# A hybrid attention layer: the stick-breaking heads' weights transposed by VectorE squares and a round trip through DRAM instead of by TensorE

## The chip, the cores and the metric

The kernel runs on one core of one Trainium2 chip. The metric is the device time of one execution in microseconds (us); lower is better. The core has TensorE (PE in the profile, its weight loads PEld), VectorE (DVE), ScalarE (ACT), GpSimd (POOL) and SyncE (SP). Each engine works through its own instructions in the order in which they stand in the built program, and starts one when the semaphores that it waits for have been raised. SP computes nothing: it issues nearly all DMAs of this kernel, in order.

## The reference: what is computed

One residual layer over a sequence of 1024 positions with 1024 channels. The input is normalised and modulated, projected to queries, keys, values and gates of 16 heads of 64 channels (8 forgetting heads, 8 stick-breaking heads), each head mixes, the gated head outputs go through one output projection, and a residual and a layer norm end it. Cut to the part that the change touches:

```python
def _stick_breaking_block(q, k, v, q_pos, k_pos):
    scale = HEAD_DIM ** -0.5
    z = jnp.einsum('bhqd,bhkd->bhqk', q, k).astype(jnp.float32) * scale
    strict = k_pos[None, :] < q_pos[:, None]
    log_beta = jax.nn.log_sigmoid(z)
    log_keep = jnp.where(strict, jax.nn.log_sigmoid(-z), 0.0)
    later = lax.cumsum(log_keep, axis=3, reverse=True) - log_keep
    w = jnp.where(strict, jnp.exp(log_beta + later), 0.0)
    return jnp.einsum('bhqk,bhkd->bhqd', w.astype(v.dtype), v)
```

The weights `w` come out with the queries on the partitions; the product with `v` sums over keys, so it needs the keys on the partitions. Each 128x128 block of `w` must be transposed.

## The kernel before, in words

Everything is fp32 split into a high part (fp32r) and a low remainder, and a product is made of high and low terms. After a start that computes modulation and the first projections, the program is a list of 128 units `u = (p, h, i)`: head pair `p` of 0 to 7 (0 to 3 are the stick-breaking heads), head `h` of the pair, and block `i` of 128 queries, which sees `(i + 1) * 128` keys (`ke`). This stretch of 64 stick-breaking units, from the first scores at 88.8 us to the last, is called the stage here.

One stick-breaking unit goes through these steps (line numbers are those of the profile of before):

- `att_scores`: the scores `S` on PE (L427, L428), into one PSUM tile that has no second buffer; `kp` and `be`, two sigmoids on ACT (L447, L448); a running product from the right over `kp` on DVE (L453, and L457 for more than 512 keys); the product `be * kp` on POOL (L461). `kp` and `be` are SBUF tiles of one pool of six buffers, so three units can hold theirs at a time.
- `att_transpose`, called LAG = 2 units later: for each group `g` of up to four key blocks, the blocks of `be` are transposed by PE into a PSUM tile `T` (L478), ACT copies it to the high part `hi` (L480, the "cast" of this text), and DVE subtracts to get the low part `lo` (L481).
- `att_pv`, when both units of a pair of query blocks (2j, 2j+1) are there: the product with `v` on PE (L493), the sum of its halves by ACT and DVE (L512, L513), the gate on POOL (L514), and a store to `y_dr` issued by SP (L522).

Between the units PE works on "fillers": the projections of the next pairs (L270 to L272 for queries, keys and gates, L327 to L329 for values), cut in small steps and dealt out evenly over the units by the table FILL. PE's order is written out by hand: within `pe_order` every PE instruction stands where the program's loop puts it. The orders of ACT, DVE, POOL and SP are made by a scheduler that simulates a timeline. SP issues in this stage the loads of the weights for the fillers (`raw`, L121), the copies of the keys to the other half of the partitions (L252), and the stores of `y_dr` (L522).

The loop that sets the order:

```python
    for k in range(len(units) + LAG + 1):
...
                att_scores(units[k], units[k + 1] if k + 1 < len(units) else None)
...
        fill(want[2 * k + LEAD + 1])
        while ready:
            att_pv(*ready.pop(0))
        if LAG <= k < len(units) + LAG:
            u = units[k - LAG]
            att_transpose(u)
```

Of the kernel before, what the change touches and what calls it, by code (L numbers as in the profile page):

```python
# [27 lines left out]
def tile_hybrid_layer(  # L28
# [17 lines left out]
    nc = tc.nc  # L46
# [4 lines left out]
    dr = ctx.enter_context(tc.tile_pool(name="dr", bufs=1, space=bass.MemoryType.DRAM))  # L51
# [39 lines left out]
    causal = cp.tile([P, P], F32, tag="causal", name="causal")  # L91
# [17 lines left out]
    y_dr = dr.tile([NPAIR, P, SEQ], F32, tag="y_dr", name="y_dr")  # L109
    wo_dr = dr.tile([2, NPAIR, P, D], F32, tag="wo_dr", name="wo_dr")  # L110
    f_dr = dr.tile([8, SEQ], F32, tag="f_dr", name="f_dr")

    def raw_tile(name):
        return sb.tile([P, 528], F32, tag="wraw", bufs=2, name=name)
# [129 lines left out]

    def evac_k(p, ch, acc, kst, klo, heads):
        s = slice(ch * 512, ch * 512 + 512)
        for h in heads:
            r = slice(h * HD, h * HD + HD)
            o = slice((1 - h) * HD, (1 - h) * HD + HD)
            first = nc.scalar.copy(kst[h][r, s], acc[r, :])  # L250
            kf = kst[h].bitcast(F32)
            nc.sync.dma_start(kf[o, s], kf[r, s])  # L252
            if p not in CASTS_FIRST:
                last = nc.vector.tensor_tensor(klo[r, s], acc[r, :], kf[r, s], op=ALU.subtract)
        if p in CASTS_FIRST:
            for h in heads:
                r = slice(h * HD, h * HD + HD)
                last = nc.vector.tensor_tensor(klo[r, s], acc[r, :], kst[h].bitcast(F32)[r, s], op=ALU.subtract)  # L258
        return first, last

    def evac_g(p, ch, acc, sg):
# [12 lines left out]
    qst, kst, klo, sgt, vt = {}, {}, {}, {}, {}  # L274
# [91 lines left out]
    def forget_rows(lf):  # L366
        scratch = att_tile("fscratch")
        tri, fr = scratch[:, :P], scratch[:64, P:2 * P]
        nc.gpsimd.memset(tri, 1.0)
        nc.gpsimd.affine_select(out=tri, in_=tri, pattern=[[1, P]], base=0,  # L370
                                channel_multiplier=-1, compare_op=ALU.is_ge, fill=0.0)
        fp = t_tile("fcum")
        nc.tensor.matmul(fp[:, 64:129], ones.to_broadcast([P, P]), flf, start=True, stop=True)
        nc.tensor.matmul(fp[:, :64], tri, lf, start=True, stop=True)
        pre = fsb.rearrange("p h t -> p (h t)")
        nc.vector.tensor_tensor_scan(pre, fp[:, 64:128], later.rearrange("p h t -> p (h t)"), initial=0.0,
                                     op0=ALU.add, op1=ALU.mult)
# [6 lines left out]
        nc.sync.dma_start(f_dr.rearrange("h (t p) -> (h t) p", p=P), fr)  # L384
        yield

    fb = {}
# [7 lines left out]
    floor, ps_causal = [], []  # L395
# [11 lines left out]
    def att_causal(u):  # L407
        p, h, i = u
        if p >= 4:
            f = fb[2 * (p - 4) + h]  # L410
            dg = slice(i * P, i * P + P)
            nc.vector.tensor_tensor(f[:, dg], f[:, dg], ps_causal[0][:, :P] if ps_causal else causal, op=ALU.add)

    def att_scores(u, following):
        p, h, i = u
        z = zq.pop(u)
        ke = (i + 1) * P
        ns = 1 if ke <= 512 else 2
        w = ke // ns
        qs = slice(i * P, i * P + P)  # L420
        dg = slice(ke - P, ke)
        if p >= 4:
            f = fb[2 * (p - 4) + h]
        S = s_tile(f"S_{p}_{h}_{i}")
        for s in range(ns):
            ks = slice(s * w, s * w + w)
            nc.tensor.matmul(S[:, s, :w], qst[p][h][:, qs], kst[p][h][:, ks], start=True, stop=False)  # L427
            nc.tensor.matmul(S[:, s, :w], z, klo[p][:, ks], start=False, stop=True)  # L428
        v3 = lambda a: a[:, :ke].rearrange("p (a b) -> p a b", a=ns)
        if p >= 4:  # L430
            a = att_tile(f"a_{p}_{h}_{i}")
            nm = sb.tile([P, 1], F32, tag="nm", bufs=4, name=f"nm_{p}_{h}_{i}")
            l = sb.tile([P, 1], F32, tag="l", bufs=4, name=f"l_{p}_{h}_{i}")
            rows = nc.vector.tensor_tensor_reduce(out=v3(a), in0=S[:, :ns, :w], in1=v3(f),  # L434
                                           op0=ALU.add, op1=ALU.min, scale=-1.0, scalar=BIG,
                                           accum_out=nm)
# [5 lines left out]
            nc.gpsimd.tensor_scalar(a[:, :ke], a[:, :ke], l, 1.0, op0=ALU.mult, op1=ALU.mult)  # L442
            st_w[u] = a
        else:
            kp = att_tile(f"kp_{p}_{h}_{i}")
            be = att_tile(f"be_{p}_{h}_{i}")
            nc.scalar.activation(v3(kp), S[:, :ns, :w], AF.Sigmoid, scale=-1.0)  # L447
# [5 lines left out]
            scan = nc.vector.tensor_tensor_scan(rv, rv, floor[0][:, 512 - n:][:, ::-1], initial=0.0,  # L453
                                                op0=ALU.mult, op1=ALU.max)
            if ke > n:
                rv = kp[:, :ke - n][:, ::-1]
                scan = nc.vector.tensor_tensor_scan(rv, rv, floor[0][:, 0:1].to_broadcast([P, ke - n]),  # L457
                                                    initial=kp[:, ke - n:ke - n + 1], op0=ALU.mult, op1=ALU.max)
            with after(scan):
                att_causal(following)  # L460
            nc.gpsimd.tensor_tensor(be[:, :ke - 1], be[:, :ke - 1], kp[:, 1:ke], op=ALU.mult)  # L461
            nc.gpsimd.memset(be[:, ke - 1:ke], 0.0)
            st_w[u] = be

    def att_transpose(u):
        p, h, i = u
# [638 lines left out]
```

## Time and profile before

| | |
|---|---|
| median of 3 runs | 685.24 us (685.07 to 685.33) |
| the profiled execution | 685.25 us, span of its trace 683.5 us |
| PE, PEld busy | 98 %, 86 % of the span |
| DVE, ACT, POOL busy | 66 %, 56 %, 63 % |
| granted TensorE clock, mean | 0.999 |
| DMA moved | 81.60 MB, mean 119 GB/s |
| the stage of the 64 stick-breaking units | about 88.8 to 342.9 us |

Busy time is that of instructions at work; waiting, semaphores and the issuing of DMAs do not count. PE's matmuls overlap in the pipeline, so the duration of one is longer than what it adds in a row of many. A row of the timeline gives start, duration, engine, line, operation, what it writes and reads, and in brackets how long the engine had been idle and which instruction released it. A DMA row has the time that SP needs to issue it, and its landing is when the semaphore is raised that tells of its data.

### The profile page before, as it was taken

Reading aid. Unit: us, or ns where it says so; the run is one execution under the profiler, and the core shown is the slowest. Engines: PE = TensorE matmul, PEld = TensorE weight load, DVE = VectorE, ACT = ScalarE, POOL = GpSimd, SP = SyncE. Lnnn points to the kernel's source line nnn. Section 1 sums busy time; section 2 is a strip of 40 time slices with the busy share of each in tenths; the row PEclk is TensorE's granted clock in tenths of the full one; section 3 lists DMA queues with packets and bytes.
Section 4 is the critical chain, followed back from the end, with each engine's and each line's share of the span. In section 5 each row is a group of like instructions: output and inputs, shape, how many; then the busy total and the mean of one; then the engine's idle time right before and its main releaser. Section 6 shows DMA issues by size and latency. Waiting matters only on the chain.

```text
span 683.5 us, 11770 instructions
## 1 busy us (share of the span) xinstructions
PE 667.2 (98%) x4021; PEld 587.2 (86%) x4021; DVE 450.6 (66%) x914; ACT 382.0 (56%) x861; POOL 427.7 (63%) x558
## 2 busy tenths in 40 slices
PE   5999999999999999999999999999999999999995
PEld 4789898888998888889988888899988889888885
DVE  6785368867666667676675665765566677774645
ACT  5668357856567666566675564655565667531000
POOL 5558977756348566556388896877584364665411
PEclk9999999999999999999999999999999999999999
DMA  9966231112102121122144563453341298143301
GB/s 338 410 236 233 82 105 44 41 29 60 29 9 86 27 57 54 37 55 55 55 131 136 172 176 121 143 166 129 101 150 40 72 327 318 58 162 118 123 31 62
DMA packets 45036, 81.60 MB, mean 119 GB/s; under 512 B 5232, under 2 KB 18864, under 8 KB 44976
## 3 DMA queue, kind: packets, MB, share of 16 engines
q1 hardware_dynamic: 43536, 76.63, 33.8%
q10 hardware_dynamic: 1440, 4.21, 2.2%
q8 instruction: 32, 0.52, 0.3%
q14 instruction: 28, 0.23, 0.1%
HBM read 60.34 MB, written 16.29 MB: 112 GB/s over the span
## 4 chain that ended last, share of the span: by engine, by line
PE 94%; DMA 3%; DVE 2%; ACT 0%; issue 0%; POOL 0%; DVEq 0%
PE m L270 10%; PE m L272 10%; PE m L271 10%; PE pv L493 10%; PE T L478 9%; PE S L428 5%; PE S L427 5%; PE o L884 4%; PE o L882 4%; PE o L883 4%; PE v L327 4%; PE v L328 4%; PE v L329 4%; DMA raws<-in_w_qkg_dram 2%; PE st_late L589 1%; PE st_q L589 1%
## 5 line engine op out<-in xcount | busy, mean ns | idle before, releaser
L270 PE MATMUL m<-uh,whi 128*128 128x512 f32 x304 | 126.4, 416 | 0.0
L272 PE MATMUL m<-uh,wlo 128*128 128x512 f32 x304 | 119.7, 394 | 0.0
L271 PE MATMUL m<-ul,whi 128*128 128x512 f32 x304 | 119.7, 394 | 0.0
L481 DVE TENSOR_TENSOR pt<-T,pt 128x512 fp32r<-128x512 f32 (+2 forms) x192 | 100.5, 550 | 17.5 <-ACT pt L480 16.5
L461 POOL TENSOR_TENSOR be<-be,kp 128x127 f32<-128x127 f32 (+3 forms) x64 | 77.2, 1207 | 33.1 <-DVE kp L457 23.5
L480 ACT CAST pt<-T 128x512 fp32r<-128x512 f32 (+2 forms) x192 | 85.8, 480 | 16.1 <-PE T L478 12.5
L453 DVE TENSOR_TENSOR_SCAN kp<-kp,floor 128x512 f32<-128x512 f32 (+2 forms) x64 | 65.2, 1018 | 31.2 <-ACT kp L447 30.1
L493 PEld LDWEIGHTS pv<-pt,v 128*128 128x128 f32 (+1 forms) x640 | 77.1, 163 | 4.4 <-DVE pt L481 0.7
L493 PE MATMUL pv<-pt,v 128*128 128x256 f32 (+3 forms) x640 | 80.4, 271 | 0.5 <-DVE pt L481 0.5
L442 POOL TENSOR_SCALAR a<-a,l 128x1024 f32<-128x1024 f32 (+3 forms) x64 | 48.1, 751 | 40.3 <-DVE l L441 26.7
L272 PEld LDWEIGHTS m<-uh,wlo 128*128 128x128 f32 x304 | 57.1, 188 | 13.6
L440 ACT ACTIVATE a<-a,nm 128x1024 f32<-128x1024 f32 (+3 forms) x64 | 49.8, 778 | 33.8 <-DVE nm L434 32.7
L427 PE MATMUL S<-k,q 128*128 128x512 f32 (+5 forms) x192 | 66.5, 348 | 0.2 <-DVE nm L434 0.2
L428 PE MATMUL S<-kl,qz 128*128 128x512 f32 (+5 forms) x192 | 65.5, 342 | 0.0
L270 PEld LDWEIGHTS m<-uh,whi 128*128 128x128 f32 x304 | 57.3, 188 | 8.5 <-DVE kl L258 0.2
L271 PEld LDWEIGHTS m<-ul,whi 128*128 128x128 f32 x304 | 57.4, 189 | 8.0
L434 DVE CUSTOM_DVE_ANT_0 a<-S,fb 128x1024 f32<-128x1024 f32 (+3 forms) x64 | 48.3, 755 | 20.1 <-PE S L428 9.3
L514 POOL TENSOR_TENSOR ty<-ty,sg 64x256 f32<-64x256 f32 x64 | 47.5, 742 | 22.3 <-DVE ty L513 11.1
L447 ACT ACTIVATE kp<-S 128x128 f32<-128x128 f32 (+3 forms) x64 | 41.7, 652 | 31.6 <-PE S L428 29.4
L327 PE MATMUL v<-whi_v,uh 128*128 128x256 f32 (+1 forms) x192 | 56.0, 292 | 0.0
L405 ACT CAST qz<-q 64x128 fp32r<-64x128 f32 x128 | 37.4, 295 | 33.2 <-PE S L428 31.8
L328 PE MATMUL v<-whi_v,ul 128*128 128x256 f32 (+1 forms) x192 | 54.2, 282 | 0.0
(285 smaller groups left out, 1593.6 us busy)
## 6 DMA issues: line engine op xcount, KB each, us to landing
raw<-in_w_qkg_dram SPq DMA_DIRECT2D x38, 256.0 KB, 2.9
wss<-in_w_ss_dram SPq DMA_DIRECT2D x16, 512.0 KB, 8.4
x<-in_x_dram SPq DMA_DIRECT2D x8, 512.0 KB, 6.9
k<-k SPq DMA_DIRECT2D x32, 128.0 KB, 2.3
wg<-in_w_gate_dram SPq DMA_DIRECT2D x8, 512.0 KB, 4.9
raw_o<-in_w_out_dram SPq DMA_DIRECT2D x16, 256.0 KB, 2.8
fb<-f_dr ACTq DMA_DIRECT2D x8, 512.0 KB, 4.3
wo_dr<-whi_o SPq DMA_DIRECT2D x16, 256.0 KB, 2.5
```

Source lines behind the costliest of these rows:

```text
L270: nc.tensor.matmul(acc, hi[:, c], u_hi[kt][:, s], start=(kt == 0), stop=False)
L271: nc.tensor.matmul(acc, hi[:, c], u_lo[kt][:, s], start=False, stop=False)
L272: nc.tensor.matmul(acc, lo[:, c], u_hi[kt][:, s], start=False, stop=(kt == NB - 1))
L327: nc.tensor.matmul(acc[:, :n], u_hi[kt][:, ts_], hi[:, s], start=(kt == 0), stop=False)
L328: nc.tensor.matmul(acc[:, :n], u_lo[kt][:, ts_], hi[:, s], start=False, stop=False)
L427: nc.tensor.matmul(S[:, s, :w], qst[p][h][:, qs], kst[p][h][:, ks], start=True, stop=False)
L428: nc.tensor.matmul(S[:, s, :w], z, klo[p][:, ks], start=False, stop=True)
L453: scan = nc.vector.tensor_tensor_scan(rv, rv, floor[0][:, 512 - n:][:, ::-1], initial=0.0, op0=ALU.mult, op1=ALU.max)
L461: nc.gpsimd.tensor_tensor(be[:, :ke - 1], be[:, :ke - 1], kp[:, 1:ke], op=ALU.mult)
L480: nc.scalar.copy(hi[:, :n, qo:qo + P], t3)
L481: nc.vector.tensor_tensor(lo[:, :n, qo:qo + P], t3, hi.bitcast(F32)[:, :n, qo:qo + P], op=ALU.subtract)
L493: nc.tensor.matmul(acc[:m, q0:256], vt[p][:, kb, h * P:h * P + m], pt[:, kb % 4, q0:], start=start, stop=stop)
```

## The change

For the stick-breaking pairs (`on_dma(p)`, p < 4) the weights no longer go through PE. In `att_scores`, after the product on POOL, DVE transposes `be` into `kp` in squares of 32x32 within the 128 rows, and writes them ordered by the square's column within a block. Then `through_dram` has SP store `kp` in a DRAM tile `far` (one DMA of 128 rows; four such tiles), and read it back into `be` with four DMAs, one for each group of 32 partitions, in such an order that each square row lands on its partition. In `att_transpose` ACT casts `hi` straight from `be` in SBUF, and the remainder `lo` is subtracted by DVE for the first four key blocks (g = 0) and by POOL for the others (g = 1). The 288 transposes of `be` on PE are gone; the 288 of the forgetting pairs stay. LAG, FILL and the pools are as before. A second function, `quartered(p)`, asks for p >= 4 and p < 4 at once and is never true, so the branches that hang on it are left out here.

```diff
+    def by_blocks(t, n, natural):
+
+        return t[:, :n * P].rearrange("p (k s c) -> p k s c" if natural else "p (s k c) -> p k s c", k=n, s=4)
+
+    def on_dma(p):
+        return p < 4
...
+        moved = on_dma(p)
...
             nc.gpsimd.tensor_tensor(be[:, :ke - 1], be[:, :ke - 1], kp[:, 1:ke], op=ALU.mult)
             nc.gpsimd.memset(be[:, ke - 1:ke], 0.0)
+            if moved:
+                nc.vector.transpose(by_blocks(kp, i + 1, False), by_blocks(be, i + 1, True))
+                through_dram(u, kp, be)
             st_w[u] = be
+
+    def through_dram(u, src, dst):
+
+        p, h, i = u
+        ke, run = (i + 1) * P, (i + 1) * 32
+        far = dr.tile([P, SEQ], F32, tag="far", bufs=4, name=f"far_{p}_{h}_{i}")
+        nc.sync.dma_start(far[:, :ke], src[:, :ke])
+        for s in range(4):
+            nc.sync.dma_start(dst[s * 32:s * 32 + 32, :ke].rearrange("k (q r) -> k q r", q=4),
+                              far[:, s * run:s * run + run].rearrange("(q k) r -> k q r", q=4))
 
     def att_transpose(u):
         p, h, i = u
...
             hi, lo = st_pt[p, h, j, g]
+            if on_dma(p):
+                full = a[:, :(i + 1) * P].rearrange("p (q k c) -> p k q c", q=4, c=32)[:, 4 * g:4 * g + n]
+                parts = [t[:, :n, qo:qo + P].rearrange("p k (q c) -> p k q c", q=4)
+                         for t in (hi, hi.bitcast(F32), lo)]
+                nc.scalar.copy(parts[0], full)
+                eng = nc.gpsimd if p >= 4 or g else nc.vector
+                eng.tensor_tensor(parts[2], full, parts[1], op=ALU.subtract)
+                continue
             tp = t_tile(f"T_{p}_{h}_{i}_{g}")
```

How the built program moves, at three places.

SP, in the first head of pair 3, around units i = 2 to 4. Before, it issues stores of `y_dr`, loads of weights (`raw`) and copies of keys (`k`):

```order
L121 DMA raw_v_3_3693<-in_w_v_dram 128x512
L522 DMA y_dr<-ty_1_3_3433 64x256
L121 DMA raw_2_0_4188<-in_w_qkg_dram 128x512
L522 DMA y_dr<-ty_0_0_3517 64x256
L252 DMA k_0_3502<-k_0_3502 64x512
L252 DMA k_1_3503<-k_1_3503 64x512
L522 DMA y_dr<-ty_0_1_3605 64x256
```

In the changed program (its L526 is the store to `far`, L528 the four reads back, the middle numbers of a name are head and block) the same stretch reads:

```order
L132 DMA raw_v_3_3768<-in_w_v_dram 128x512
L528 DMA be_0_1_3426<-far_0_1_3433 32x4x64 x4
L526 DMA far_0_2_3472<-kp_0_2_3464 128x384
L528 DMA be_0_2_3465<-far_0_2_3472 32x4x96 x4
L596 DMA y_dr<-ty_1_3_3502 64x256
L526 DMA far_0_3_3528<-kp_0_3_3520 128x512
L132 DMA raw_2_0_4271<-in_w_qkg_dram 128x512
L528 DMA be_0_3_3521<-far_0_3_3528 32x4x128 x4
L596 DMA y_dr<-ty_0_0_3595 64x256
L526 DMA far_0_4_3573<-kp_0_4_3564 128x640
L276 DMA k_0_3580<-k_0_3580 64x512
L528 DMA be_0_4_3565<-far_0_4_3573 32x4x160 x4
```

The four reads of a unit stand right behind its own store, or behind it and one to four other DMAs, and the next unit's store behind them.

ACT, in the same place, around the sigmoids of unit i = 3 (kp_0_3). Before, the cast (L480) reads the PSUM tile `T`:

```order
L480 CAST pt_2_1_3_1_3343<-T_1_7_1_3385 128x4x128
L241 ACTIVATE q_1_3291<-m_0_0_3292 64x512
L447 ACTIVATE kp_0_2_3402<-S_0_2_3399 128x384
L448 ACTIVATE be_0_2_3403<-S_0_2_3399 128x384
L405 CAST qz_80<-q_0_2686 64x128
L512 COPY ty_1_3_3433<-pv_1_3_3416 64x256
L480 CAST pt_3_0_0_0_3438<-T_0_0_0_3440 128x128
L447 ACTIVATE kp_0_3_3453<-S_0_3_3450 128x512
```

In the changed program the cast (L545) reads `be`, that is, what the reads from DRAM brought:

```order
L501 ACTIVATE be_0_2_3465<-S_0_2_3461 128x384
L435 CAST qz_80<-q_0_2744 64x128
L545 CAST pt_2_1_3_0_3408<-be_1_7_3318 128x4x128
L545 CAST pt_2_1_3_1_3412<-be_1_7_3318 128x4x128
L545 CAST pt_3_0_0_0_3507<-be_0_0_3370 128x128
L545 CAST pt_3_0_0_0_3507<-be_0_1_3426 128x2x128
L586 COPY ty_1_3_3502<-pv_1_3_3485 64x256
L500 ACTIVATE kp_0_3_3520<-S_0_3_3517 128x512
```

The casts of units 7, 0 and 1 now stand together ahead of the sigmoid of unit 3, where before unit 1's stood behind it.

PE, in the first head of pair 3 after the product of units 4 and 5 (pv_0_2). Before, the transposes of unit 6 follow it, and then fillers (v):

```order
L493 MATMUL pv_0_2_3725<-pt_3_0_2_1_3620,v_1979 64x256
L493 MATMUL pv_0_2_3725<-pt_3_0_2_1_3619,v_1979 128x256
L478 MATMUL T_0_6_0_3745<-ident,be_0_6_3581 128x128 x4
L478 MATMUL T_0_6_1_3754<-ident,be_0_6_3581 128x128 x3
L327 MATMUL v_0_3712<-whi_v_2_3689,uh_116 128x256
```

In the changed program the fillers follow at once:

```order
L567 MATMUL pv_0_2_3807<-pt_3_0_2_1_3698,v_2030 64x256
L567 MATMUL pv_0_2_3807<-pt_3_0_2_1_3697,v_2030 128x256
L352 MATMUL v_0_3794<-whi_v_2_3764,uh_116 128x256
L353 MATMUL v_0_3794<-whi_v_2_3764,ul_124 128x256
L354 MATMUL v_0_3794<-wlo_v_2_3765,uh_116 128x256
```

The transposes are gone, and nothing else of PE's order moves: the product still stands behind the scores of the unit after its pair.

More of the change, by code (lines that the diff above doesn't have):

```diff
@@ L246, in evac_k, with made, home @@
         s = slice(ch * 512, ch * 512 + 512)
+        def made(t, r):
+            return t[r, :].rearrange("p (k s c) -> p k s c", k=4, s=4) if quartered(p) else t[r, :]
+        def home(t, r):
+            if not quartered(p):
+                return t[r, s]
+            return t[r, :].rearrange("p (s k c) -> p k s c", s=4, c=32)[:, 4 * ch:4 * ch + 4]
         for h in heads:
@@ L383, in forget_rows @@
         nc.scalar.copy(fr, ft)
-        nc.sync.dma_start(f_dr.rearrange("h (t p) -> (h t) p", p=P), fr)
+        if quartered(4):
+            for hh in range(8):
+                nc.sync.dma_start(f_dr[hh].rearrange("(s t c) -> t s c", s=4, c=32),
+                                  fr[8 * hh:8 * hh + 8, :].rearrange("t (s c) -> t s c", s=4))
+        else:
+            nc.sync.dma_start(f_dr.rearrange("h (t p) -> (h t) p", p=P), fr)
         yield
@@ L441, in att_scores @@
             nc.vector.reciprocal(l, l)
[L442 removed]
+            if moved:
+                nc.scalar.activation(a[:, :ke], a[:, :ke], AF.Copy, scale=l)
+                nc.vector.transpose(a[:, :ke], a[:, :ke])
+                through_dram(u, a, a)
+            else:
+                nc.gpsimd.tensor_scalar(a[:, :ke], a[:, :ke], l, 1.0, op0=ALU.mult, op1=ALU.mult)
             st_w[u] = a
```

41 lines of the change are left out of this document (33 added, 8 removed).

## The prediction

> **What bounds the kernel now.** I read the page first: its busy time by engine, and the chain of work that ended last.
>
> ```profile
> PE 667.2 (98%) x4021; PEld 587.2 (86%) x4021; DVE 450.6 (66%) x914; ACT 382.0 (56%) x861; POOL 427.7 (63%) x558
> PE 94%; DMA 3%; DVE 2%; ACT 0%; issue 0%; POOL 0%; DVEq 0%
> ```
>
> PE is busy nearly all the time and carries 94 % of the chain. Then the busy time by stage, for head pair 0 and for pairs 1 to 3 (columns: window, its length, then busy time and instructions of PE, PEld, DVE, ACT, POOL, then granted clock, DMA share, GB/s).
>
> ```profile
> 88.80:138.00 49.20, 47.73 (x321) 43.24 (x320) 39.27 (x63) 37.33 (x86) 35.28 (x51) 1.00 0.19 52
> 138.00:342.90 204.90, 204.90 (x1331) 185.69 (x1331) 139.46 (x234) 132.15 (x299) 117.64 (x164) 1.00 0.17 47
> ```
>
> The stage takes 49.2 + 204.9 = 254.1 us for 64 units: 3.1 us per unit in pair 0, which has half the fillers, and 4.3 in the others. PE does not pause in pairs 1 to 3, so whatever leaves PE there is gained, as long as nothing else becomes later than PE. DMA is at 17 to 19 % and is no limit by bandwidth.
>
> **What is removed from PE.** The first row is the line of the transposes, the others are pieces of the chain, where a piece has only the time that is its own.
>
> ```profile
> L478 PE MATMUL T<-ident,be x288: 270/272/299, 94.3 to 355.0; 128*128 128x128 f32 x144
> 313.95 0.77 PE T L478 x7
> 317.79 0.87 PE T L478 x8
> ```
>
> One transpose lasts 272 ns, but eight in a row cost the chain 0.87 us, 0.109 us each. So 288 x 0.109 = 31.4 us leave PE, and PE needs 254.1 - 31.4 = 222.7 us for the stage: 2.5 us per unit in pair 0 and 3.8 in the others. [...]
>
> **What is added on DVE and POOL.**
>
> ```profile
> L481 DVE TENSOR_TENSOR pt<-T,pt 128x512 fp32r<-128x512 f32 x96 | 64.6, 686 | 16.8 <-ACT pt L480 16.3
> L453 DVE TENSOR_TENSOR_SCAN kp<-kp,floor 128x512 f32<-128x512 f32 x40 | 48.8, 1219 | 24.3 <-ACT kp L447 23.7 <-issue 0.2
> L126 POOL TENSOR_TENSOR wlo<-raw,whi 128x512 fp32r<-128x512 f32 x38 | 49.1, 1297 | 2.4 <-DMA wo_dr<-wlo_o 0.8
> L480 ACT CAST pt<-T 128x512 fp32r<-128x512 f32 x96 | 54.8, 587 | 7.7 <-PE T L478 5.0
> ```
>
> No row shows a transpose on DVE. Per 512 columns it lies between a plain pass (0.69 us) and a scan (1.22). I take the plain pass, since it too handles each element once: the 288 blocks are 72 times 512 columns, 49 us (88 at the other end). The remainders of the second group move to POOL, 32 instructions of 320 columns in the mean: 14 us less on DVE, 26 us more on POOL's 153, which has room. DVE then has 179 - 14 + 49 = 214 us of work in the stage, 253 at the other end; against 222.7 that is already close to PE. ACT's casts keep their number.
>
> **What is added on SP, the part that I think decides.** Five DMAs per unit are added to the one or so that it has. First what an issue costs, then what landing costs (the list of DMA issues: KB each, median us from issue to landing).
>
> ```profile
> 0.79 1.80 SPq L145 DMA_DIRECT2D x<-in_x_dram  x4
> L252 SPq DMA_DIRECT2D k<-k x32: 461/477/589, 44.8 to 547.7; - x32
> L859 SPq DMA_DIRECT2D yr<-y_dr x16: 359/371/480, 509.8 to 642.0; - x16
> ```
>
> ```profile
> y_dr<-ty SPq DMA_DIRECT2D x56, 64.0 KB, 1.9
> wo_dr<-whi_o SPq DMA_DIRECT2D x16, 256.0 KB, 2.5
> wo_dr<-wlo_o SPq DMA_DIRECT2D x16, 256.0 KB, 2.2
> xr<-in_x_dram SPq DMA_DIRECT2D x8, 512.0 KB, 3.4
> k<-k SPq DMA_DIRECT2D x32, 128.0 KB, 2.3
> ```
>
> Four issues in a row take 1.80 us, 0.45 each; the strided `yr` 0.37, the half-height `k` 0.48. For the four reads, which are strided and of quarter height, I take 0.45 (0.37 to 0.53). The store of a unit has 64 to 512 KB. It lands 1.9 us after its issue at 64 KB, 2.2 to 2.5 at 256; 512 KB I put at 2.9 by an estimate between that and `xr`. The mean is 2.35 (2.0 to 3.0). A read has up to 128 KB and lands in 2.3 us as `k` does.
>
> By the order, the reads of a unit stand behind its own store and wait for its landing, and all else on SP waits with them: the next unit's store first of all, then stores of `y_dr`, for which nobody waits, and loads of filler weights, which are issued a filler ahead and which I let cost nothing. So SP's time per unit is 2.35 + 4 x 0.45 = 4.15 us, plus other DMAs that don't fit into the wait. In 11 of the 64 units the store stands one unit earlier and its wait is saved. Counted from the order for the first head of pair 3: seven waits of 2.35 (16.5), one store without wait (0.45), 32 reads (14.4), five other issues behind reads (2.25), and about 2 us in which SP stands because a unit's weights aren't ready: the cast of unit 1 stands ahead of the sigmoid of unit 3. That is 35.6 us for eight units, against 34.2 before (204.9 / 6), and 24.6 in pair 0 (49.2 / 2). Eight heads take 285 us, 4.5 us per unit. It is over PE's 2.5 and 3.8, so SP would pace the stage and PE would wait.
>
> A second count, the path of one unit, gives the same direction. These are the steps of a unit with i = 7, and the start of its product.
>
> ```profile
> 307.16 0.40 PE L428 MATMUL S<-kl,qz 128*128 128x512 f32 x1
> 311.34 2.00 POOL L461 TENSOR_TENSOR be<-be,kp 128x1023 f32<-128x1023 f32 x1 [0.49 <-DVE kp L457]
> 321.70 1.96 PE L493 MATMUL pv<-pt,v 128*128 128x256 f32 x16
> ```
>
> From the end of the scores (307.56) to the end of POOL's product (313.34) are 5.8 us. Then: DVE 1.4, store 2.9, three more issues and the last read 1.35 + 2.3, two casts 1.2, the remainder on POOL 1.3: 16.3 us. The product stood 14.1 us behind the scores, of which 1.6 were transposes that go: 12.5. So the large units come 4 us late at PE even if no queue were busy; and the scores behind the late product, and the sigmoids behind a waiting cast on ACT, come late with it.
>
> **The sum.** Stage 285 instead of 254.1: +31 us. The 31.4 us that leave PE are no gain any more, since they become PE's waiting. Before and behind the stage nothing changes: PE's order differs in the 288 transposes alone, so the change also does what it says. The profiled execution took 685.25 us, 1.75 over its span, and the median of the runs is 685.24; so 685.25 + 31 = 716, rounded with the few waits not counted to **717**. With reads at 0.37 and stores at 2.0 a head takes 14 + 0.4 + 11.8 + 1.9 + 2 = 30 us, 241 in all, 672; with 0.53 and 3.0 it is 21 + 0.5 + 17 + 2.7 + 2 = 43 us, 346 in all, 777.
>
> **The rivals.**
>
> *Hidden everywhere.* The round trip is ahead of PE in every unit and the stage takes PE's 222.7 us: 654 us. For it: the weights of unit 7 now lie ready 4.4 us before their transposes (313.34 and 317.79), a slack that the new way can use. Against: SP must be under 2.5 us per unit in pair 0, less than one store's landing with its four issues even at the low ends (3.5). Chance 0.05.
>
> *Hidden in pairs 1 to 3 only.* This is the case on the other side. It decides below 3.8 us per unit on SP, which 0.37 per read, 2.0 per store and no standing would give (28.1 / 8 = 3.5). Pairs 1 to 3 then take PE's 204.9 - 216 x 0.109 = 181.4 us, pair 0 16 x 3.5 = 56: 237, so 17 less than now: 668 us. For it: the low ends are in the rows, and the 11 saved waits. Against: DVE, at 214 of work in 237, would be nearly as full. Chance 0.12.
>
> *More than SP: queues behind queues.* A cast that waits on ACT holds sigmoids and evacuations of PSUM behind it, and the remainders on DVE hold scans. A unit's way from scores to cast is 10.7 us in the mean: 3.9 to the end of POOL's product (1.9 for i = 1 by the rows below, 5.8 for i = 7), DVE 0.8, store 2.35, issues 1.35, read 2.3. If it also waits for one unit's SP time (4.5), that becomes 15.2. In the order of ACT a unit's cast stands three sigmoids of `kp` back in the mean, so a unit takes 15.2 / 3 = 5.1 us: 64 are 325, 756 us.
>
> ```profile
> 282.56 0.29 PE L428 MATMUL S<-kl,qz 128*128 128x256 f32 x1
> 284.13 0.64 POOL L461 TENSOR_TENSOR be<-be,kp 128x255 f32<-128x255 f32 x1 [0.38 <-DVE kp L453]
> ```
>
> The clock could do the same, since PE would now wait:
>
> ```profile
> 675.00:680.00 5.00, 1.65 (x15) 1.45 (x13) 3.14 (x7) 0.55 (x1) 1.24 (x3) 1.00 0.00 0
> 680.00:683.50 3.50, 0.00 (x0) 0.00 (x0) 0.57 (x2) 0.00 (x0) 0.19 (x1) 0.71 0.41 150
> ```
>
> At the kernel's end PE stops, and in the last 3.5 us the granted clock is 0.71. At that clock PE's 222.7 us become 314: 745. Against it: my stalls are mostly shorter, and in the five microseconds before, with PE idle for 3.35, the clock is 1.00. [...] Chance of queues and clock together 0.25.
>
> **How the numbers follow.** Forecast 0.56 (its own range 696 to 745), hidden everywhere 0.05, hidden in three pairs 0.12, queues or clock 0.25; 0.02 is left for a stage that comes out as before, between the second rival and the forecast. Within 0.2 % (1.4 us) is what a measurement here can't tell from no change. Faster 0.05 + 0.12 = 0.17, same 0.02, slower 0.81. The range from 668 to 772 leaves out the first rival, the lower part of the second, and a tail of about 0.08 above.
>
> **What would show it.** Right: in the changed trace PE has waits in the stage whose releaser is ACT or DVE at `pt`, the stage is about 285 us, SP issues a unit's five DMAs every 4.5 us with stores landing at 1.9 to 2.9 us, and pair 0 stretches most (49 to about 71 us). Wrong: PE at 98 % or more in pairs 1 to 3 (then the round trip is hidden), reads issued under 0.4 us, a granted clock below 0.95 in the stage, or DVE busy over nine tenths there (then DVE is the pace).

## The result and the profile after

The changed kernel takes **760.4 us** (median of 4 runs, 759.5 to 764.5) against 685.2 (685.07 to 685.33): 1.111 times as long, 95 % interval 1.107 to 1.115. The forecast was 717 with a range from 668 to 772. The direction and the range held, but the loss of 75 us is more than twice the 32 that were forecast.

First the page of the changed kernel: busy time, the granted clock in 40 slices, and the chain of work that ended last.

```profile
PE 674.7 (89%) x3733; PEld 578.4 (76%) x3733; DVE 497.9 (66%) x946; ACT 385.0 (51%) x861; POOL 466.6 (62%) x590
...
PEclk9999998899999799999898899999999999999999
...
PE 57%; DMA 18%; SPq 6%; DVE 6%; ACT 5%; issue 4%; POOL 4%; ACTq 0%; POOLq 0%; DVEq 0%
DMA be<-far 8%; DMA far<-kp 7%; PE pv L567 7%; SPq L528 6%; PE m L295 5%; PE m L296 5%; PE m L297 5%; PE o L958 4%; PE o L956 4%; PE o L957 4%; PE T L552 4%; PE S L472 3%; PE S L473 3%; PE v L352 2%; PE v L353 2%
```

PE has its 288 transposes less (3733 instructions instead of 4021) and yet is 7.5 us longer busy: its other work takes 39 us more, at a mean granted clock of 0.953 instead of 0.999. A third of the chain, which was 94 % PE, is now DMA, SP, DVE and ACT. Next the stage by head pairs (window, length, busy time and instructions of PE, PEld, DVE, ACT, POOL, granted clock, DMA share, GB/s). The boundaries are the ends of the scores of the units that open pairs 1, 2 and 3; the last window runs on past the last scores of the stage, which end at 406.4, until PE has stood 8.0 us ahead of the first unit behind it.

```profile
88.80:160.00 71.20, 51.77 (x268) 44.22 (x266) 48.37 (x72) 37.67 (x84) 42.14 (x57) 0.86 0.49 143
160.00:241.50 81.50, 70.86 (x425) 62.03 (x424) 58.33 (x95) 45.68 (x106) 46.48 (x59) 0.96 0.50 146
241.50:324.60 83.10, 68.39 (x314) 55.49 (x314) 59.67 (x78) 46.89 (x97) 54.55 (x72) 0.92 0.54 159
324.60:418.00 93.40, 70.66 (x411) 60.96 (x410) 63.76 (x94) 46.06 (x108) 51.47 (x65) 0.90 0.51 154
```

Pair 0 takes 71 us instead of 49, as forecast; pairs 1 to 3 take over 80 each instead of 68. No engine is full: PE is busy 262 of 329 us, DVE 230. The spans differ by 757.7 - 683.5 = 74.2 us. Of these, 63.5 lie ahead of the end of the last scores (406.4 instead of 342.9) and the other 11 behind it, most of them in that wait of PE: the loss is that of the stage. Who waits there for whom, first for all engines, then for PE and for SP alone (us in total, times, longest):

```profile
ACT pt L545 <- DMA be<-far: 82.9, 42, 6.5
DVE pt L547 <- ACT pt L545: 48.4, 33, 4.4
...
POOL be L514 <- DVE kp L510: 33.3, 22, 2.5
```

```profile
PE pv L567 <- ACT pt L545: 31.3, 17, 4.4
PE S L472 <- ACT be L501: 21.8, 11, 8.0
PE pv L567 <- DVE pt L547: 9.2, 11, 2.2
```

```profile
SPq L528 <- DMA far<-kp: 65.4, 47, 4.5
SPq L526 <- DVE kp L517: 37.1, 23, 5.2
SPq L596 <- POOL ty L588: 10.5, 11, 2.4
```

ACT's casts wait for the reads, DVE's remainders wait for the casts, PE waits for both. SP, which I had taken for the pace, itself stands 37 us until DVE has the squares ready: that speaks against it, and the runs below decide. One unit shows the round. It is the second half of the path of unit (2, 0, 7), in the chain of waits of the changed kernel (start, length, what):

```profile
290.54 0.03 DVE kp L517
290.57 1.14 issue
...
292.25 3.09 DMA far<-kp
295.33 0.02 issue
295.35 0.33 SPq L528
295.68 0.05 issue
295.73 0.44 SPq L528
...
296.68 2.98 DMA be<-far
299.67 0.02 issue
299.69 0.63 ACT pt L545
300.31 0.04 issue
300.36 3.48 PE pv L567 x16
```

From the start of its squares to its cast are 9.15 us (290.54 to 299.69), where the forecast's steps for i = 7 give 1.4 + 2.9 + 1.35 + 2.3 = 7.95. Its scores end at 281.5, though, so POOL's product is ready 9.0 us after them, not 5.8. The trip itself was sized about right, and what lies ahead of it was not.

### The profile page after: what moved, and what is told of

It is laid out like the page before. It is cut to its first block, busy times and chain, and to the rows that moved or that the text cites. A ratio compares the mean times of both kernels' runs of the same rounds, so it can differ in the third digit from the quotient of the medians.

```text
span 757.7 us, 12067 instructions
## 1 busy us (share of the span) xinstructions
PE 674.7 (89%) x3733; PEld 578.4 (76%) x3733; DVE 497.9 (66%) x946; ACT 385.0 (51%) x861; POOL 466.6 (62%) x590
## 4 chain that ended last, share of the span: by engine, by line
PE 57%; DMA 18%; SPq 6%; DVE 6%; ACT 5%; issue 4%; POOL 4%; ACTq 0%; POOLq 0%; DVEq 0%
DMA be<-far 8%; DMA far<-kp 7%; PE pv L567 7%; SPq L528 6%; PE m L295 5%; PE m L296 5%; PE m L297 5%; PE o L958 4%; PE o L956 4%; PE o L957 4%; PE T L552 4%; PE S L472 3%; PE S L473 3%; PE v L352 2%; PE v L353 2%
## 5 line engine op out<-in xcount | busy, mean ns | idle before, releaser
L567 PE MATMUL pv<-pt,v 128*128 128x256 f32 (+3 forms) x640 | 96.8, 298 | 45.6 <-ACT pt L545 31.6
L567 PEld LDWEIGHTS pv<-pt,v 128*128 128x128 f32 (+1 forms) x640 | 86.0, 181 | 59.5 <-ACT pt L545 38.5
L296 PE MATMUL m<-ul,whi 128*128 128x512 f32 x304 | 121.8, 401 | 0.0
L514 POOL TENSOR_TENSOR be<-be,kp 128x127 f32<-128x127 f32 (+3 forms) x64 | 80.1, 1252 | 47.1 <-DVE kp L510 33.3
L545 ACT CAST pt<-be 128x512 fp32r<-128x512 f32 (+2 forms) x96 | 45.7, 511 | 90.4 <-DMA be<-far 87.6
L472 PE MATMUL S<-k,q 128*128 128x512 f32 (+5 forms) x192 | 69.1, 361 | 22.1 <-ACT be L501 21.8
L547 DVE TENSOR_TENSOR pt<-be,pt 128x512 fp32r<-128x512 f32 (+2 forms) x64 | 54.8, 858 | 51.0 <-ACT pt L545 50.4
L488 ACT ACTIVATE a<-a,nm 128x1024 f32<-128x1024 f32 (+3 forms) x64 | 49.8, 778 | 32.1 <-DVE nm L482 31.4
L472 PEld LDWEIGHTS S<-k,q 128*128 128x128 f32 x192 | 37.3, 194 | 32.7 <-ACT be L501 27.6
L517 DVE STREAM_TRANSPOSE kp<-be 128x128 f32<-128x128 f32 (+3 forms) x64 | 48.7, 767 | 18.4 <-POOL be L514 14.0
L555 DVE TENSOR_TENSOR pt<-T,pt 128x512 fp32r<-128x512 f32 (+1 forms) x96 | 50.5, 553 | 10.6 <-ACT pt L554 10.3
```

The lines of the kernel that those rows point to most:

```text
L296: nc.tensor.matmul(acc, hi[:, c], u_lo[kt][:, s], start=False, stop=False)
L472: nc.tensor.matmul(sp, qst[p][h][:, qs], kh, start=True, stop=False)
L547: eng.tensor_tensor(parts[2], full, parts[1], op=ALU.subtract)
L555: nc.vector.tensor_tensor(lo[:, :n, qo:qo + P], t3, hi.bitcast(F32)[:, :n, qo:qo + P], op=ALU.subtract)
L567: nc.tensor.matmul(acc[:m, q0:256], vt[p][:, kb, h * P:h * P + m], pt[:, kb % 4, q0:], start=start, stop=stop)
```

## The experiments

In the diffs `-` is the changed kernel, or the experiment named, and `+` the experiment. Unless a range is given, a time is one execution, and the kernel before took 685.0 to 685.2 on the same chip. Executions of one kernel lay up to 7.5 us apart (749.7 to 757.2 for one of them, 759.5 to 764.5 for the changed kernel), so a difference of that size between single executions is not read.

### Is it the trip, or SP that issues it?

**Without the trip.** The squares stay, and the casts read what DVE wrote into `kp`, so the squares are not moved between groups of partitions.

```diff
-                through_dram(u, kp, be)
-            st_w[u] = be
+            st_w[u] = kp if moved else be
```

> Left out: the store to DRAM and the four reads; the casts read the tile that VectorE's square transpose wrote, so the weights are not fully transposed. PE's transposes stay gone, VectorE's stay in. Every theory in which the round trip is the cause (SP's pace, or the waiting of queues on its landing) expects the stage to fall to PE's need of 223 to 240 us, so 654 to 672 us in all. If VectorE's transposes or the remainders moved to POOL were the cause, it stays above 700.

Measured: 695.4 us. Neither theory had this: without the DMAs of the trip the change still costs 10 us, 41 more than PE's bound of 654. So there is a second loss that has nothing to do with DRAM.

**The trip beside the work.** Store and reads are issued, the casts still read `kp`; the data that comes back isn't used.

```diff
-            st_w[u] = be
+            st_w[u] = kp if moved else be
```

> Left out: the use of what comes back. Store and reads are issued as in the changed kernel, but the casts read the tile that VectorE wrote; be is still held until the reads have landed, kp until the store has. If SP's pace is the cause (4.5 us per unit in five issues and a wait), nothing of that is taken away: 720 to 745 us. If the waiting of casts on the landing, and of everything queued behind the casts on ACT, VectorE, POOL and PE, is the cause, it falls to 660 to 700 us.

Measured: 712.5 us, between the two ranges. SP issues and waits for the same DMAs as in the changed kernel, and yet the scores of one unit follow those of the last by 4.34 us in the mean (273.6 us for 63 steps), where they do so by 5.02 in the changed kernel. So it isn't SP's own work that sets 5.02. Of the 65 us between the kernel without trip (695.4) and the changed one, the trip that nobody waits for costs 17. Part of that is `be`, which can't be overwritten until the reads have landed in it: the profile of this run has this wait of ACT's next sigmoid.

```profile
ACT be L501 <- DMA be<-far: 11.1, 14, 2.0
```

**Two more DMAs for SP.** Two small copies within DRAM, written in the program behind the reads of each unit.

```diff
+        for x_ in range(2):
+            spare_dr = dr.tile([P, 8], F32, tag="spare", bufs=16, name=f"spare_{p}_{h}_{i}_{x_}")
+            nc.sync.dma_start(spare_dr, c_t)
```

> As the changed kernel, with two more small DMAs per unit on SP behind the reads (4 KB DRAM to DRAM each, nobody waits for them), some 0.9 us of SP time per unit. If SP's pace is the cause, the stage grows by 64 x 0.9 = 58 us: about 818 us. If the length of a unit's way with three units in flight is the cause, they only fill gaps of SP in which it waits for VectorE, and delay the next store at times: 765 to 790 us.

Measured: 767.7 us, 7 more, inside the second expectation. But the run doesn't test what it was meant to test. The copies wait for nothing of a unit, and the scheduler, which makes SP's order, put them early. Here are their first and last start:

```profile
L532 SPq DMA_DIRECT2D spare<-in_c_t_dram x128: 488/587/1288, 13.3 to 211.3; - x128
```

Of the 128, 72 stand ahead of the stage (before 88.8), 56 in its first 122 us, and none behind. The first scores end 6.6 us later than in the changed kernel (96.7 instead of 90.1), which is about as much as the whole difference. So the run says nothing of SP's pace in pairs 2 and 3. In pair 0, where 33 of the copies stand with 18 us of issuing, the stretch from the first unit's scores to those of pair 1 takes 82.1 us instead of 70.0; whether that is SP's pace or the backlog of the start stays open.

That SP doesn't pace the stage rests on the two runs around this one: on the same trip at 4.34 us per unit, above, and on the fourth unit in flight, below.

**A warm PE.** Six matmuls whose result nobody reads, ahead of each product of the stage.

```diff
+            if on_dma(p):
+                warm = t_tile(f"warm_{p}_{h}_{j}")
+                for _ in range(6):
+                    nc.tensor.matmul(warm, u_hi[0][:, :P], u_hi[0][:, :512], start=True, stop=True)
```

> As the changed kernel, with six idle matmuls (128x512, about 0.23 us each, 44 us in all) on PE ahead of each product of the stage, so that PE works where it waited and its clock stays granted. If the clock (0.86 to 0.92 in the stage) is a main cause, the time falls to 735 to 748 us and the granted clock of the stage rises to 0.97 or more. If it isn't, the time stays within 10 us of 760 or grows by part of the 44 us.

Measured: 749.5 us at a mean clock of 0.983 instead of 0.953, between the two expectations. So some 11 of the 75 us (760.4 - 749.5) are put down to the clock, as far as one execution tells; the waiting itself is the larger part.

### How much is too few units in flight?

**Four units in flight**, and as a control **three, with the same buffers**. The six buffers of one size are split, four for `kp` and two for `be`, so there are still six, and the reads land in `kp`. Both move the loading of two bias rows behind the last stick-breaking unit.

```diff
-        return big("att", 6, name, dt)
+        return big("atb", 2, name, dt) if second else big("att", 4, name, dt)
...
-                through_dram(u, kp, be)
-            st_w[u] = be
+                through_dram(u, kp, kp)
+            st_w[u] = kp if moved else be
...
-    LAG = 2
+    LAG = 3
```

> Four units in flight instead of three (the casts of a unit stand behind the scores of the third unit after it), whole trip kept. So that SBUF holds it, the weights' six buffers are split: four for kp, two for be, and the four reads land in kp, not be. Units in flight theory: a unit's path from the end of its scores to its cast is 14.9 us on average in the changed kernel, and the stage runs at 14.9/3 = 5.0 us a unit; with four in flight 14.9/4 = 3.7 us a unit, below what PE (3.8 us) and the untransported chain (695 us without a trip) need, so about 695 to 720 us. SP theory (SP's issues and its waits in order set the pace, however many are in flight): 745 to 765 us, no change.

> The control for the one with four units in flight: the same split of the buffers and the same place for the reads to land (kp instead of be), but three units in flight as in the changed kernel. Both theories: 750 to 775 us; a part above 760 would be what be's two buffers cost, a part below what the earlier free be is worth.

Measured: 732.0 us with four in flight (731.9 to 733.5, ratio to before 1.069, 1.067 to 1.071), 752.9 with three. The fourth unit is worth 21 us. If SP were the pace it would be worth nothing, since SP has the same DMAs to issue; but 732 is outside both expectations, 12 above the top of the one that was nearer. Unit by unit, from the end of the last score matmul to the start of the first cast, the path is 15.05 us in the mean over the 64 units of the changed kernel, and the scores of one unit follow those of the last by 5.02 us: three paths overlap. A path measured like this holds its own waits, so 15.05 / 3 alone says no more than that three units are in flight all the time; that a fourth helps shows that it was too few. With four in flight the path is 15.8 us, which would give 3.95 us a unit, but 4.57 are taken. Something else binds there.

**Four units in flight, no trip.** The last one without its trip.

```diff
-                through_dram(u, kp, kp)
```

> The squares on VectorE kept, no trip through DRAM (the casts read what VectorE wrote into kp), and four units in flight. If the 695 us with three in flight come from the path (scores, sigmoids, scans, product, squares, cast, one behind the other on engines that wait for each other), 655 to 672 us, with TensorE the bound again. If they come from VectorE's amount of work (224 us of 254 busy in the stage), 685 to 697 us.

Measured: 702.8 us, above both expectations. With only two buffers `be` becomes the wait, so this run doesn't decide what holds the kernel without a trip at 695:

```profile
ACT be L501 <- DVE kp L518: 25.8, 13, 5.9
```

### What costs 41 us without the trip?

**No squares either.** The kernel without a trip, and now nothing transposes in the stage; casts and remainders read `be` as POOL left it.

```diff
-            if moved:
-                nc.vector.transpose(by_blocks(kp, i + 1, False), by_blocks(be, i + 1, True))
-            st_w[u] = kp if moved else be
+            st_w[u] = be
```

> Nothing transposes at all in the stage: no squares on VectorE, no trip, no TensorE transposes; the casts and remainders read be as POOL's product left it (the weights are used untransposed). What is left of the change is the TensorE time taken away and the remainders of g = 1 on POOL. Against 695 us with the squares and without the trip: if the squares' 49 us in VectorE's queue are what keeps that at 695, 652 to 672 us (685 less 31, plus a little); if it is POOL with the remainders, or the casts behind them, 685 to 697 us.

Measured: 684.8 us, at the foot of the second expectation. Of the kernel before, 288 transposes have been taken away and nothing put in their place, and it is no faster. What is left of the change is where the remainders stand, and what the casts and they read: SBUF now, PSUM before. These are the remainders of 512 columns on DVE in the kernel before and in the changed one, from 88.8 to 410 us (count | busy us, mean ns | idle before):

```profile
L481 DVE TENSOR_TENSOR pt<-T,pt 128x512 fp32r<-128x512 f32 x58 | 38.8, 684 | 8.6 <-ACT pt L480 8.3
```

```profile
L547 DVE TENSOR_TENSOR pt<-be,pt 128x512 fp32r<-128x512 f32 x37 | 34.2, 926 | 33.4 <-ACT pt L545 33.3
```

The same in the kernel without trip and in the one without squares as well:

```profile
L546 DVE TENSOR_TENSOR pt<-kp,pt 128x512 fp32r<-128x512 f32 x40 | 48.5, 1211 | 2.8 <-ACT pt L544 2.5
```

```profile
L544 DVE TENSOR_TENSOR pt<-be,pt 128x512 fp32r<-128x512 f32 x40 | 42.3, 1057 | 7.8 <-ACT pt L542 7.4
```

The mean rose from 0.68 us to between 0.93 and 1.21. The timeline of the changed kernel shows how, DVE first, then POOL in the same microseconds (start, length, instruction):

```profile
321.66 2.23 DVE L547 TENSOR_TENSOR pt<-be,pt 128x512 fp32r<-128x512 f32 x1 [0.23 <-ACT pt L545]
```

```profile
321.57 1.77 POOL L514 TENSOR_TENSOR be<-be,kp 128x895 f32<-128x895 f32 x1 [0.31 <-DVE kp L510]
```

```profile
328.02 1.78 DVE L547 TENSOR_TENSOR pt<-be,pt 128x512 fp32r<-128x512 f32 x1
329.73 1.23 DVE L517 STREAM_TRANSPOSE kp<-be 128x1024 f32<-128x1024 f32 x1
```

```profile
327.27 2.00 POOL L514 TENSOR_TENSOR be<-be,kp 128x1023 f32<-128x1023 f32 x1 [1.09 <-DVE kp L510]
```

In both, DVE's remainder ends 0.53 to 0.55 us after the end of a POOL instruction that had started before it (323.89 after 323.34; 329.80 after 329.27). Of the changed kernel's 37, 15 took more than 0.70 us, and ten of these end like that, 0.53 to 0.56 us after POOL; the shortest of the 37 took 0.65. I read this as a remainder that stands until POOL is through and then runs, called blocking from here on; the rows show the lengths and the ends, not the wait itself. DVE's scan of 512 columns, whose second operand is the PSUM tile `floor`, is not disturbed: 1.21 us in the mean in the changed kernel, 1.22 before, and none over 1.22 although 20 of the 40 ran beside a tensor instruction of POOL. That points at the second operand. The next four runs test it.

**VectorE's remainders read PSUM**, in the changed kernel, in the one without trip, in the one without squares, and with four in flight. The second operand is `floor`; `lo` then holds no true remainder. The remainders of the last three units (four, with four in flight) stay as they were.

```diff
-                eng.tensor_tensor(parts[2], full, parts[1], op=ALU.subtract)
+                if eng is nc.vector and not ps_causal:
+                    fl = floor[0][:, :n * P].rearrange("p (k q c) -> p k q c", k=n, q=4)
+                    eng.tensor_tensor(parts[2], parts[1], fl, op=ALU.subtract)
+                else:
+                    eng.tensor_tensor(parts[2], full, parts[1], op=ALU.subtract)
```

> The changed kernel with its whole trip, but VectorE's remainders take as second operand a PSUM tile (the scan's floor) in place of the transposed weights in SBUF; they still wait for the cast. So lo holds no true remainder; the count and size of all instructions is unchanged. Why: in the changed kernel the 512-column remainder on VectorE, with both operands in SBUF, takes 0.65 to 2.2 us, 0.67 to 0.69 where POOL is idle beside it and 1.28 in the median where a POOL tensor operation covers it, while before, with one operand in PSUM, it took 0.66 to 0.69 always. Blocking theory (VectorE with two SBUF operands waits out POOL's instruction): no remainder over 0.7 us, 9 us less in those of 512 columns and 8 us in the others, 735 to 752 us. If the blocking is hidden behind the trip's latency: 755 to 762 us.

> The kernel without a trip (casts read what VectorE's squares wrote), with VectorE's remainders reading PSUM in place of the weights, as in the one before. Its remainders of 512 columns took 1.21 us in the mean against 0.68. Blocking theory: some 27 us less on VectorE, 665 to 680 us against 695. If it is VectorE's squares alone that hold the 695: 688 to 697 us.

> The kernel without squares and without a trip (684.8 us, no faster than before although TensorE has 31 us less to do), with VectorE's remainders reading PSUM in place of the weights. Blocking theory: 15 us less in the 512-column remainders and 10 in the shorter ones, 655 to 668 us, TensorE the bound again. If POOL's own added remainders or the casts behind POOL's product hold it: 680 to 686 us.

> Four units in flight (732 us with the whole trip) and VectorE's remainders reading PSUM. If the two costs, too few units in flight for the trip's latency and VectorE's blocking by POOL, are separate and add up: 705 to 718 us. If with more in flight the blocking is hidden: 728 to 733 us.

| remainders read | SBUF | PSUM | difference |
|---|---|---|---|
| no squares, no trip | 684.8 | 669.2 | -15.7 |
| squares, no trip | 695.4 | 675.8 | -19.6 |
| four in flight, whole trip | 732.0 | 717.2 | -14.8 |
| the changed kernel | 760.4 | 751.7 | -8.7 |

The last row is of timed runs: 751.7 us, 749.7 to 757.2, ratio 1.098 (1.092 to 1.103), below the changed kernel's 1.107 to 1.115. The remainders of 512 columns without squares and without trip, now from PSUM; and all lengths of the changed kernel with this edit, with the shortest, median and longest in ns:

```profile
L546 DVE TENSOR_TENSOR pt<-pt,floor 128x512 fp32r<-128x512 f32 x37 | 24.6, 664 | 1.0 <-ACT pt L542 1.0
```

```profile
L549 DVE TENSOR_TENSOR pt<-pt,floor x61: 259/686/689, 100.9 to 402.6; 128x512 fp32r<-128x512 f32 x37, 128x128 fp32r<-128x128 f32 x8, 128x256 fp32r<-128x256 f32 x8, 128x384 fp32r<-128x384 f32 x8
```

None of the changed remainders is over 0.69 us any more. The three remainders that were left as they were are a control within the run; in the kernel without squares and without trip they read:

```profile
L548 DVE TENSOR_TENSOR pt<-be,pt 128x512 fp32r<-128x512 f32 x3 | 5.9, 1955 | 0.2 <-ACT pt L542 0.2
```

So one operand decided it: 1.96 us in the mean with both in SBUF, 0.66 with one in PSUM, in the same run. The edit also frees `be` for the next unit one instruction earlier, but that is not the gain: in the kernel without squares nothing waited for a remainder in order to reuse `be`, and in the changed one ACT did once, for 0.5 us. POOL gains too: without squares its 64 products took 1.32 us in the mean beside remainders from SBUF, and 1.21 beside those from PSUM, as before the change (1.21). The blocking is shown as a length that goes with the operand, and it is worth 9 to 20 us, least where the engines wait for the trip anyway. Expected were 735 to 752, 665 to 680, 655 to 668 and 705 to 718: three inside, the third 1 us above.

**All remainders on VectorE.** The run without squares and without blocking, POOL now relieved of the second group.

```diff
-                eng = nc.gpsimd if p >= 4 or g else nc.vector
+                eng = nc.vector
```

> The kernel without squares and trip, with VectorE's remainders reading PSUM (669 us), and now all remainders on VectorE, the second group too, so that POOL has only what it had before. If POOL's added 27 us are what lies between 669 and TensorE's 654: 652 to 660 us. If it is the path of casts and remainders behind POOL's product: 666 to 673 us.

Measured: 669.8 us, inside the second expectation. The remainders moved to POOL are not what lies between 669 and 654. PE's row of the page says part of it, with two of its waits, in the kernel without squares, trip or blocking:

```profile
PE 641.7 (96%) x3733; PEld 558.5 (84%) x3733; DVE 437.5 (66%) x882; ACT 384.4 (58%) x862; POOL 453.1 (68%) x590
...
PE S L472 <- ACT be L501: 3.3, 6, 1.0
PE fcum L399 <- POOL fscratch L395: 2.8, 1, 2.8
```

PE's busy time fell from 667.2 to 641.7, by 25.5 us. That is not the price of the transposes: in the trace of before, the 288 add 31.8 us to PE's busy time (from the end of the instruction before each to its own end), 0.110 each. But the rest of PE's work takes 6.3 us longer now, at a clock of 0.992 instead of 0.999, and PE stands 667.5 - 641.7 = 25.8 us in its span instead of 16.3. So of the 31.8 us that left PE, 16 came out: the other 16 are PE's new waits and the slower work beside them.

### Would a mixture win?

**Only some units by DRAM**: the four small ones of each head in pairs 1 to 3, or every fourth. The other units are transposed by PE as before.

```diff
-    def on_dma(p):
-        return p < 4
+    def on_dma(p, i=0):
+        return 0 < p < 4 and i < 4
```

In the second run the condition is `0 < p < 4 and i % 4 == 3`.

> Only the four small units (i = 0 to 3) of each head in pairs 1 to 3 take the way over VectorE and DRAM, 24 of the 64 units with 60 of the 288 blocks; the others are transposed by TensorE as before. TensorE loses 60 x 0.109 = 6.5 us. Theory of too few units in flight: the small units' paths (8 to 12 us) fit into three units of 4.2 us, nothing waits, and what is lost is the blocking of 24 remainders (some 0.3 us each, 7 us on VectorE, which is two thirds busy): 679 to 686 us. Theory that each unit sent costs for itself (75 + 31 us over 288 blocks or 64 units, so 1.6 us a unit before TensorE's gain): 24 x 1.6 - 6.5 = 32 us, about 717 us.

> Only the units i = 3 and i = 7 of each head in pairs 1 to 3 take the way over VectorE and DRAM: 12 units with 72 blocks, and never two in a row. TensorE loses 7.8 us. Theory of too few units in flight: a path of 11 us (i = 3) fits into three units of 4.2 us, that of i = 7 (16 us or more) comes some 4 us late six times, less what TensorE's fillers cover: 680 to 700 us. Theory that each unit sent costs for itself: 12 x 1.6 - 7.8 = 12 us, 697 us. Below 684 it would beat the kernel before.

Measured: 695.7 us (692.1 to 697.3, ratio 1.014, 1.012 to 1.016) and 708.7 (707.7 to 709.8, ratio 1.034, 1.033 to 1.036). Neither mixture wins. Both lie outside what either theory gave: the first between the two, the second above them. With PE's forecast gain added back, a small unit costs (10.6 + 6.5) / 24 = 0.7 us, one of every fourth (23.6 + 7.8) / 12 = 2.6 us, although the units beside it go through PE. Of the second price the blocking is next to nothing: the 11 remainders of DVE between 88.8 and 370 us took 0.72 us in the mean, against 0.68 before; how much it is of the first was not shown. A unit sent through DRAM need not have another behind it to do harm: its product stands at a fixed place in PE's order, and PE stops there. PE in the stage of the second run, its waits and its windows:

```profile
PE pv L567 <- ACT pt L545: 13.3, 6, 3.7
PE pv L567 <- POOL pt L547: 2.2, 3, 1.5
```

```profile
138.00:343.00 205.00, 188.40 (x1100) 165.13 (x1098) 131.67 (x212) 118.45 (x267) 116.07 (x157) 0.95 0.27 80
```

No version beat the kernel before: those that came out under it leave out the transposition or the true remainder.

## Why the prediction was wrong

Put in a row, the runs split the 75 us. Each step is the difference of two of them.

| step | us | runs |
|---|---|---|
| PE without 288 transposes, with its new waits | -16.0 | before 685.2, no squares, trip or blocking 669.2 |
| remainders read SBUF, and are longer beside POOL | +15.7 | 684.8 |
| squares in DVE's queue | +10.5 | 695.4 |
| trip issued, nobody casts from it | +17.1 | 712.5 |
| casts wait for the landing | +47.9 | 760.4 |

The order of the steps matters: taken out of the whole kernel instead, the blocking is worth 9. Some 11 us of the later steps are the clock.

- *PE loses 31.4 us.* Right as an amount of work: it was 31.8. As a gain, 16 came out, even with squares, trip and blocking left out, since PE then waits more.
- *DVE's squares take 49 us.* Right: 64 of them took 48.7, as a plain pass, in this row of the changed kernel.

```profile
L517 DVE STREAM_TRANSPOSE kp<-be 128x128 f32<-128x128 f32 (+3 forms) x64 | 48.7, 767 | 18.4 <-POOL be L514 14.0
```

- *DVE has 214 us of work.* It had 230 in the stage's 329. What was missing are the remainders on DVE, some 17 us longer in the stage. The prediction left them at the price of the PSUM row, 0.686, without a reason, though they now read SBUF.
- *Landing and issue.* Right: the store lands after 2.63 us in the mean (2.35 forecast), the last read after 2.60 (2.3), a read takes 0.43 us to issue, and one follows the other after 0.48 (0.45 forecast).
- *SP paces the stage at 4.5 us per unit.* **This step failed.** It took the engines' times for alternatives, of which the largest decides. The stage ran at 5.02 us per unit, and SP was not what set that: with the same DMAs, but casts that don't wait for them, it ran at 4.34; in the changed kernel SP itself stood 37 us for the squares; and a fourth unit in flight, which takes nothing off SP, won 21 us. In place of SP's pace stands a unit's path, waits included, shared by three units. That SP's issues cost nothing isn't shown either: four units in flight still took 4.57.
- *The path of a unit is 10.7 us in the mean.* The second failure, and what to put in place of the first. It was 15.05: 5.62 to the end of POOL's product (3.9 forecast), 0.67 of waiting and 0.77 for the squares, 0.65 waiting and 2.63 for the store, 0.40 waiting, 1.43 until the last read is issued, 2.60 until it lands, and 0.30 until the cast. The durations add up to about what was forecast. Of the 4.35 us that were missing, 3.7 are queues: 1.7 ahead of the trip, the rest the waits of DVE, SP and ACT before each step. The 1.7 don't hang on the trip: without it that stretch is as long, 5.8 us, and without squares, trip and blocking it is 4.5, against 4.0 before.
- *The rival of queues behind queues*, chance 0.25, had 15.2 / 3 = 5.1 us per unit and 756 us. The runs bear out its form, 15.05 / 3 = 5.02. That its number came so near (756 and 760) is in part luck: it had put all of the 4.5 us to waiting for SP, where waits ahead of DVE, SP and ACT, a longer start of the path and somewhat longer steps add up to 4.35. The clock was put down as another way to the same end; it came on top, with 11 us.
- *What would show it.* Of the signs against the forecast, the clock below 0.95 appeared. DVE over nine tenths did not, nor reads under 0.4 us.

Open is why PE waits 9.5 us more than before in the kernel without squares, trip or blocking (at `S` for ACT, once for POOL, and the rest is scattered), what binds four units in flight at 4.57 us each, how the 17 us of the unused trip divide between `be`, which stays taken, and SP, and why a sent unit of every fourth costs 2.6 us: its late product shows only part of it.

## What to carry to other kernels

Where a transposed or transported tile takes the place of a PSUM tile, price its readers anew: here VectorE's remainders of 512 columns, which had one operand in PSUM, took 0.68 us in the mean, with both in SBUF 0.93 to 1.21, and with one in PSUM again none took over 0.69. For a round trip count the path of one unit, with the waits in each in-order queue, and divide by the units in flight; an engine's own sum of work is only a lower bound beside that. Before work taken off an engine is counted as a gain, build the kernel with the step simply left out: here that run alone, at 685, would have said that nothing was to be won in this form. And look in the built program where an added instruction stands: most of the DMAs that were added to each unit, and that waited for nothing, ended up ahead of the stage.

## What the runs showed of the hardware that was not expected

The granted clock fell further than in the rows of before, where the lowest was 0.71. In five microseconds of the changed kernel PE was idle, and in the next five the clock was 0.50:

```profile
410.00:415.00 5.00, 0.00 (x0) 0.00 (x0) 3.25 (x6) 0.85 (x3) 3.01 (x3) 0.81 0.95 302
415.00:420.00 5.00, 2.73 (x6) 2.15 (x7) 1.21 (x2) 2.34 (x5) 3.62 (x4) 0.50 0.86 242
```

And a remainder on DVE took far longer than the longest of the changed kernel, 2.23 us: in the kernel without a trip one took 4.69 us, where none of the kernel before was over 0.69.

```profile
L546 DVE TENSOR_TENSOR pt<-kp,pt x64: 293/700/4690, 94.0 to 366.8; 128x512 fp32r<-128x512 f32 x40, 128x128 fp32r<-128x128 f32 x8, 128x256 fp32r<-128x256 f32 x8, 128x384 fp32r<-128x384 f32 x8
```
